# The attention mask as 32 extra operand columns, and PSUM banks given out in order of time

## The chip, the cores and the metric

The kernel runs on one core of one Trainium2 chip. The metric is the device time of one execution in microseconds (us), as the median of several runs; lower is better. The profile is one more execution with the hardware profiler on; its rows are what all durations here are read from. In them PE is TensorE (the matrix engine), PEld its loading of weights, DVE is VectorE, ACT is ScalarE, POOL is GpSimd, and SP is the engine that issues the DMAs.

## The reference

One layer of an encoder on 1024 tokens of width 1024: a half-step SwiGLU FFN, a mixer with two head groups (a gated MLP and an attention over low-rank latents), a second half-step FFN and a final norm.

```python
x = x + 0.5 * swiglu(rmsnorm(x, ffn1_norm), w_gate, w_up, w_down)      # hidden 2816
h = rmsnorm(x, mix_norm) @ w_in        # u 512 | v 512 | c_q 256 | c_kv 128 | k_rope 32
y_a = gmlp_mixer(u, v, ...)
y_b = mla_mixer(c_q, c_kv, k_rope, ...)                                # 8 heads, 96 wide
x = x + concat(rmsnorm(y_a), rmsnorm(y_b)) @ w_out
x = x + 0.5 * swiglu(rmsnorm(x, ffn2_norm), ...)
x = rmsnorm(x, final_norm)
```

The attention is causal in chunks of 64 tokens. A query block has 128 tokens, which is two chunks, and the mask is applied before the softmax:

```python
mask = k_chunk[None, :] <= q_chunk[:, None]
s = jnp.einsum('bqhd,bkhd->bhqk', qb, k)
s = jnp.where(mask[None, None], s, -1e30)
p = jax.nn.softmax(s, axis=-1)
```

In a query block t, keys beyond its 128 tokens are never computed. What the mask must still shut out is one quarter of the diagonal block: the first 64 queries against the last 64 keys.

## The kernel before

All matrix products run in a split form: an operand is held as a high part and a low part (names ending in h and l), and a product is three matmuls, high by high, high by low and low by high. The three lines of such a product stand beside each other in the profile (L963, L964, L965 for the scores).

The program goes through these stages, in this order of time: FFN 1 gate and up (0 to about 500 us), FFN 1 down, the input projection and the gated MLP, the latent stage, the attention (about 844 to 1035 us), the output projection, FFN 2 gate and up (from about 1127 us), FFN 2 down, final norm.

- The FFN products use a Strassen scheme. Gate and up weights come in units; a unit has products P1 to P7 (L438), whose weights are sums of weight quarters (S1 to S4, built by DVE at L409 and split at L423 on ACT and L424 on DVE) and whose moving operands are sums of token quarters (T1 to T4, B11, B21, B22, built by DVE at L368 to L373 and split at L360 on ACT and L361 on DVE). At the start of each FFN the eight token tiles are normalized (L291, DVE), transposed on PE (L286) and copied out (L350, ACT); the T sums need the last of the eight tiles.
- The latent stage (latent_tile, one per token tile of 128) makes queries (L864 to L866) and keys and values (L871 to L873), scales them on DVE (L897 to L899) and rotates the rope columns on POOL (L763 to L767, L901). The tile qn of a token tile has 8 heads by 128 columns, of which 96 are used; kn likewise.
- The attention takes one head h at a time in query pairs. head_T transposes four token tiles of a head (L947) and evicts them as qh, ql, kh, kl (L951 on ACT, L952 on DVE), with 96 rows. scores makes one query block's scores in PSUM with L963 to L965, one group of three for each 512 keys, then adds the mask with one more matmul, L966: its weights are a row of 64 ones and 64 zeros (mrow), its moving operand a row of 64 times -1e30 (mneg), both bf16, and it is added to the last 64 columns. Then DVE takes the row maximum (L968), ACT the exponential (L970), PE transposes the result (L993), which ACT and DVE split (L276, L277); weighted multiplies by the values (L1002, L1003), and folded finishes a pair of blocks (L1014, L1016).

What sets the order: the steps are written out by hand in the code, and a tile scheduler with a timeline of its own (schedule_with_timeline_sim) then places each instruction on its engine's queue, by the dependences between tiles. Each engine runs its queue in order. PSUM has 8 banks. Which bank a PSUM tile gets is fixed before that, by place: a dry pass runs through the program with a clock that counts 1 for a matmul or transpose and 0.01 for any other instruction, and notes when each tile is first and last used. In the kernel before, place takes the tiles in the order of size by lifetime and gives each the bank with the longest free gap, where gaps beyond REACH (160) count as equal and the lowest bank wins. Two tiles that follow each other in a bank are a dependence for the scheduler: the later tile's first matmul waits until the earlier tile is copied out.

## Time and profile before

| what | value |
|---|---|
| median of 3 runs | 1804.01 us (1801.94 to 1806.21) |
| the profiled execution | 1804.58 us, of which 1802.8 us span |
| PE busy | 1731.7 us, 96% of the span |
| DVE busy | 1122.5 us, 62% |
| ACT busy | 750.3 us, 42% |
| POOL busy | 124.9 us, 7% |
| mean granted clock of PE | 0.98 |

The span is the time from the first to the last instruction; 1.8 us lie around it. The granted clock is a share of TensorE's full 2.4 GHz: at 1.00 a 512-column matmul follows the one before it after 0.23 us, and in a stretch at the lower of its two levels, 1.2 GHz, after 0.43 us. A window whose mean clock is, say, 0.90 holds a piece at the lower level. A matmul's duration (0.39 us for 512 columns) is longer than this pace, since matmuls overlap; what one costs a busy PE is the step from its start to the next start.

### The profile page before, as it was taken

What the parts mean: (1) busy time and instruction counts of PE and PEld (TensorE: products, weight loads), DVE (VectorE), ACT (ScalarE), POOL (GpSimd) and SP (SyncE); (2) the same over time, 40 slices, a digit from 0 to 9 for tenths busy, and PEclk for the clock granted to TensorE, in tenths of its full rate; (3) what the DMA queues carried; (4) which work ended last, traced back from release to release, by engine and by line L of the source; (5) the groups of instructions that cost most, each with busy time, mean ns of one, the idle gap of its engine ahead of it and who ended that gap; (6) DMA issues with size and microseconds to landing.
All of it is one profiled execution on the core that took longest, in us unless ns stands there. A gap on an engine that the chain in (4) does not pass through costs nothing.

```text
span 1802.8 us, 21101 instructions
## 1 busy us (share of the span) xinstructions
PE 1731.7 (96%) x8196; PEld 1444.9 (80%) x8196; DVE 1122.5 (62%) x1481; ACT 750.3 (42%) x1139; POOL 124.9 (7%) x242
## 2 busy tenths in 40 slices
PE   6799999999999999997999999889999999999988
PEld 5688888888888888896888888668888888888876
DVE  6875466654687667458676544665556655658753
ACT  6533233334343353355666733433233333433442
POOL 2000000000000004225000500000000000000000
PEclk9899999999999999998999899989999999999999
DMA  6132423225834520300000452131323222783431
GB/s 204 59 117 88 135 93 117 88 94 210 292 129 158 192 88 20 109 13 1 1 1 7 142 174 71 53 118 58 134 101 111 88 95 87 245 308 102 158 121 47
DMA packets 123493, 199.51 MB, mean 111 GB/s; under 512 B 11008, under 2 KB 57600, under 8 KB 123392
## 3 DMA queue, kind: packets, MB, share of 16 engines
q1 hardware_dynamic: 122816, 197.11, 32.0%
q8 instruction: 64, 1.05, 0.2%
q10 hardware_dynamic: 576, 1.05, 0.2%
q14 instruction: 37, 0.30, 0.1%
HBM read 143.07 MB, written 55.05 MB: 110 GB/s over the span
## 4 chain that ended last, share of the span: by engine, by line
PE 91%; DVE 4%; ACT 2%; DMA 1%; SPq 1%; issue 1%; POOL 1%; POOLq 0%; ACTq 0%; DVEq 0%
PE psum L438 45%; PE psum L569 8%; PE psum L570 8%; PE psum L567 7%; PE psum L693 2%; PE psum L691 2%; PE psum L692 2%; PE psum L1093 2%; PE psum L1091 2%; PE psum L1090 2%; PE psum L993 2%; PE psum L963 1%; PE psum L286 1%; PE psum L1002 1%; PE psum L1003 1%; PE psum L965 1%
## 5 line engine op out<-in xcount | busy, mean ns | idle before, releaser
L454 DVE TENSOR_TENSOR P_b<-psum,P_b 128x1024 f32<-128x1024 f32 x33 | 40.3, 1222 | 62.8 <-PE psum L438 62.7
L454 DVE TENSOR_TENSOR P_a<-psum,P_a 128x1024 f32<-128x1024 f32 x33 | 40.3, 1221 | 55.6 <-PE psum L438 55.5
L968 DVE TENSOR_REDUCE nm<-psum 128x1 f32<-128x128 f32 (+3 forms) x64 | 47.8, 753 | 27.9 <-PE psum L966 19.8
L444 ACT COPY P_a<-psum 128x1024 f32<-128x1024 f32 x33 | 33.5, 1014 | 68.6 <-PE psum L438 68.6
L444 ACT COPY P_b<-psum 128x1024 f32<-128x1024 f32 x33 | 33.5, 1014 | 68.1 <-PE psum L438 68.1
L455 ACT ACTIVATE P_a<-P_a 128x512 f32<-128x512 f32 x33 | 20.9, 634 | 96.8 <-DVE P_a L454 96.5
L455 ACT ACTIVATE P_b<-P_b 128x512 f32<-128x512 f32 x33 | 20.9, 633 | 96.4 <-DVE P_b L454 96.3
L277 DVE TENSOR_TENSOR pl<-psum,ph 128x384 fp32r<-128x384 f32 (+1 forms) x80 | 48.8, 629 | 11.6 <-ACT ph L276 11.3
L970 ACT ACTIVATE p<-psum,nm 128x128 f32<-128x128 f32 (+3 forms) x64 | 47.9, 749 | 18.9 <-DVE nm L968 17.1
L963 PE MATMUL psum<-kh,qh 96*128 96x512 f32 (+2 forms) x96 | 41.4, 431 | 11.8 <-ACT qh L951 8.1
L257 POOL TENSOR_TENSOR r_fin<-ms_fin,mhalf 128x1 f32<-128x1 f32 x8 | 6.0, 754 | 643.6 <-DVE ms_fin L255 643.6
L1090 PE MATMUL psum<-woh,yh 128*128 128x512 f32 x128 | 50.5, 397 | 0.0
L1091 PE MATMUL psum<-wol,yh 128*128 128x512 f32 x128 | 50.1, 393 | 0.0
L276 ACT CAST ph<-psum 128x384 fp32r<-128x384 f32 (+1 forms) x80 | 41.6, 550 | 9.0 <-PE psum L993 7.9
L438 PE MATMUL psum<-xT2h_f,S2h_b 128*128 128x512 f32 x88 | 35.4, 402 | 10.1 <-ACT S2h_b L423 10.1
L993 PE MATMUL psum<-ident,p 128*128 128x128 f32 x288 | 43.5, 280 | 1.4 <-ACT p L970 1.2
L1002 PE MATMUL psum<-ph,vv 128*128 128x256 f32 x160 | 44.7, 305 | 0.1
L1003 PE MATMUL psum<-pl,vv 128*128 128x256 f32 x160 | 43.5, 301 | 0.3 <-DVE pl L277 0.3
L257 POOL TENSOR_TENSOR r_m<-ms_m,mhalf 128x1 f32<-128x1 f32 x8 | 5.6, 704 | 551.3 <-DVE ms_m L255 551.3
L1093 PE MATMUL psum<-woh,yl 128*128 128x512 f32 x128 | 43.5, 395 | 0.0
L438 PE MATMUL psum<-xT2l_f,S2h_a 128*128 128x512 f32 x88 | 35.1, 399 | 8.3 <-DVE xT2l_f L361 8.3
L438 PE MATMUL psum<-xT1l_f,S1h_b 128*128 128x512 f32 x88 | 34.7, 396 | 6.0 <-DVE xT1l_f L361 6.0
(519 smaller groups left out, 5717.8 us busy)
## 6 DMA issues: line engine op xcount, KB each, us to landing
raw_a<-in_ffn_w_gate SPq DMA_DIRECT2D x22, 512.0 KB, 4.2
raw_a<-in_ffn_w_up SPq DMA_DIRECT2D x22, 512.0 KB, 5.3
hd<-hS_a SPq DMA_DIRECT2D x44, 256.0 KB, 2.2
raw_b<-in_ffn_w_gate SPq DMA_DIRECT2D x22, 512.0 KB, 4.1
raw_b<-in_ffn_w_up SPq DMA_DIRECT2D x22, 512.0 KB, 5.2
hd<-hS_b SPq DMA_DIRECT2D x44, 256.0 KB, 2.2
aS_a<-hd SPq DMA_DIRECT2D x20, 512.0 KB, 3.9
wB_a<-in_ffn_w_down SPq DMA_DIRECT2D x20, 512.0 KB, 5.4
```

Of the source, the lines that this page charges most:

```text
L438: mm(o, lhs[:, 4 * m + k, :], rhs[:, k, :], start=pn in FIRST and n == 0, stop=n == 11, skip_group_check=True)
L444: nc.scalar.copy(ev[u, pn], bk)
L454: nc.vector.tensor_tensor(c, bk, c, op=ALU.add)
L567: mm(banks[t], hh[:, j, tl], dh[:, j, :], start=pn in DOWN_FIRST and c == 0 and j == 0, stop=False, skip_group_check=True)
L569: mm(banks[t], hh[:, j, tl], dl[:, j, :], start=False, stop=False, skip_group_check=True)
L570: mm(banks[t], hl[:, j, tl], dh[:, j, :], start=False, stop=c == 5, skip_group_check=True)
L993: nc.tensor.transpose(ps[:, i * P:(i + 1) * P], prs[j][:, c * P:(c + 1) * P], ident)
L1002: mm(acc[:, 0:256], mx["vv"][c][:, h, :], hi, start=i == 0, stop=False)
L1003: mm(acc[:, 0:256], mx["vv"][c][:, h, :], lo, start=False, stop=i == len(pts) - 1)
L1090: mm(pe[e], yh[:, k, :], wh[:, es], start=k == 0, stop=False)
L1091: mm(pe[e], yh[:, k, :], wl[:, es], start=False, stop=False)
L1093: mm(pe[e], yl[:, k, :], wh[:, e * 512:(e + 1) * 512], start=False, stop=k == KD - 1)
```

## The change

Two things are changed.

First, the mask. The L966 matmul goes, with its constants. Queries and keys get the 32 spare columns of their tiles filled: in token tile t, column t of the 32 holds 1 in the first 64 query tokens (0 elsewhere), and -1e30 in the last 64 key tokens (0 elsewhere). All other spare columns hold 0. A query block times a key block then adds -1e30 just where both are of the same token tile, the query in its first half and the key in its second. The columns are copied from two constants (qmark, kmark) by POOL, one copy of 128 x 8 x 32 for each qn and each kn: 16 copies, and four memsets at the start. The transposes of head_T, their evictions and the score matmuls work on 128 rows rather than 96; their count and their free sizes stay.

Second, the PSUM banks. place gives them out to the PSUM tiles in the order of first use, and the gap is not cut at REACH: a tile gets the bank that has been free longest. SBUF is placed as before.

PE has 8070 instructions where it had 8198, POOL 264 where it had 247; DVE, ACT and SP have as many as before. Line numbers of the changed kernel are higher by 3 up to the latent stage, by 5 to 7 behind it.

```diff
@@ place: the bank map @@
-def place(bufs, blocks, grain):
+def place(bufs, blocks, grain, in_time=False):
...
     reach = np.full(n, REACH)
     order = sorted(range(n), key=lambda i: (-size[i] * (last[i] - first[i] + 30.0), i))
+    if in_time:
+        reach[:] = 1e9
+        order.sort(key=lambda i: (first[i], i))
...
-        self.at = {"sb": place(dry.bufs["sb"], floats // GRAIN, GRAIN), "ps": place(dry.bufs["ps"], 8, 1)}
+        self.at = {"sb": place(dry.bufs["sb"], floats // GRAIN, GRAIN), "ps": place(dry.bufs["ps"], 8, 1, True)}
@@ constants @@
-    mrow = nc.const([1, P], "mrow", BF16)
-    nc.gpsimd.memset(mrow, 0.0)
-    nc.gpsimd.memset(mrow[:, 0:64], 1.0)
-    mneg = nc.const([1, 64], "mneg", BF16)
-    nc.gpsimd.memset(mneg, -1e30)
+    spare = P - DQ
+    qmark, kmark = (nc.const([P, NT * spare], n) for n in ("qmark", "kmark"))
+    for mark, half, v in ((qmark, slice(0, 64), 1.0), (kmark, slice(64, P), -1e30)):
+        nc.gpsimd.memset(mark, 0.0)
+        nc.gpsimd.memset(mark[half, 0:(NT - 1) * (spare + 1) + 1:spare + 1], v)
@@ latent_tile @@
-        q_t = tile_([P, H, P], f"qn{t}", F32)[:, :, 0:DQ]
-        k_t = tile_([P, H, P], f"kn{t}", F32)[:, :, 0:DQ]
+        q_all = tile_([P, H, P], f"qn{t}")
+        k_all = tile_([P, H, P], f"kn{t}")
+        q_t, k_t = q_all[:, :, 0:DQ], k_all[:, :, 0:DQ]
+        for a, mark in ((q_all, qmark), (k_all, kmark)):
+            m = mark[:, t * spare:(t + 1) * spare].unsqueeze(1)
+            nc.gpsimd.tensor_copy(a[:, :, DQ:P], m.to_broadcast([P, H, spare]))
...
-        mx["q"][t], mx["k"][t], mx["vv"][t] = q_t, k_t, v_t
+        mx["q"][t], mx["k"][t], mx["vv"][t] = q_all, k_all, v_t
@@ head_T @@
-            mx["qk", h] = [tile_([DQ, S], f"{n}{h}", F32R) for n in ("qh", "ql", "kh", "kl")]
+            mx["qk", h] = [tile_([P, S], f"{n}{h}", F32R) for n in ("qh", "ql", "kh", "kl")]
...
-                nc.tensor.transpose(ps[0:DQ, i * 512 + t * P:i * 512 + (t + 1) * P], src[4 * half + t][:, h, :], ident)
+                nc.tensor.transpose(ps[:, i * 512 + t * P:i * 512 + (t + 1) * P], src[4 * half + t][:, h, :], ident)
...
-            pv = ps[0:DQ, i * 512:(i + 1) * 512]
-            nc.scalar.activation(hi[:, cs], pv, AF.Copy, scale=col[0:DQ])
-            nc.vector.scalar_tensor_tensor(lo[:, cs], pv, col[0:DQ], f(hi[:, cs]), op0=ALU.mult, op1=ALU.subtract)
+            pv = ps[:, i * 512:(i + 1) * 512]
+            nc.scalar.activation(hi[:, cs], pv, AF.Copy, scale=col)
+            nc.vector.scalar_tensor_tensor(lo[:, cs], pv, col, f(hi[:, cs]), op0=ALU.mult, op1=ALU.subtract)
@@ scores @@
-            last = n <= c0 + 512
...
-            mm(ps[:, cs], ql[:, tl], kh[:, cs], start=False, stop=not last)
-        mm(ps[:, n - 64:n], mrow, mneg, start=False, stop=True)
+            mm(ps[:, cs], ql[:, tl], kh[:, cs], start=False, stop=True)
```

On PE, in the attention (head 3 in both; L963 to L966 before are L969 to L971 after; p and ident are the transposes of the softmax), a query block of the kernel before:

```order
L963 MATMUL psum<-kh_7553,qh_7549 128x384
L964 MATMUL psum<-kl_7555,qh_7549 128x384
L965 MATMUL psum<-kh_7553,ql_7552 128x384
L966 LDWEIGHTS mrow
L966 MATMUL psum<-mneg,mrow 128x64
L993 MATMUL psum<-ident,p_6_7816 128x128
L993 MATMUL psum<-ident,p_7_7829 128x128
L993 MATMUL psum<-ident,p_6_7816 128x128
```

and of the changed kernel:

```order
L969 MATMUL psum<-kh_7569,qh_7565 128x384
L970 MATMUL psum<-kl_7571,qh_7565 128x384
L971 MATMUL psum<-kh_7569,ql_7568 128x384
L954 MATMUL psum<-ident,qn_7181 128x128
L954 MATMUL psum<-ident,qn_7358 128x128
L954 MATMUL psum<-ident,qn_7424 128x128
L954 MATMUL psum<-ident,qn_7492 128x128
```

The weight load and matmul of the mask stood between the scores and the next transposes, and are gone; the key and query transposes have 128 rows.

On PE, at the start of FFN 1, the transposes of token tiles 6 and 7 (xn_f_381 and xn_f_401) in the kernel before, tile 6's at place 53 of the queue and tile 7's here, among unit 1's matmuls (A11h_a_258):

```order
L438 MATMUL psum<-xB21h_f_226,A12h_a_337 128x512
L438 MATMUL psum<-xB21l_f_227,A12h_a_337 128x512
L286 MATMUL psum<-ident,xn_f_401 128x128 x8
L438 MATMUL psum<-xB11h_f_218,A11h_a_258 128x512
L438 MATMUL psum<-xB11l_f_219,A11h_a_258 128x512
```

and in the changed kernel, where the two tiles are xn_f_384 and xn_f_404:

```order
L289 MATMUL psum<-ident,xn_f_384 128x128 x8
L289 MATMUL psum<-ident,xn_f_404 128x128 x8
L441 MATMUL psum<-xB21h_f_229,A12h_a_340 128x512
L441 MATMUL psum<-xB21l_f_230,A12h_a_340 128x512
L441 MATMUL psum<-xB21h_f_229,A12l_a_343 128x512
```

Tile 7's eight transposes were at place 77, behind 23 of unit 1's matmuls, and are at place 54 now, right behind tile 6's.

On DVE, at the same place, from the first T sum (L368) on; P_a_458 is unit 1's product P1 plus P2, and xB22l and xT2l are the low parts of the B22 and T2 operands. Before:

```order
L368 TENSOR_TENSOR t_f_462<-b_f_314,b_f_310 128x1024 x2
L369 TENSOR_TENSOR t_f_465<-t_f_462,b_f_153 128x1024
L373 TENSOR_TENSOR b_f_310<-b_f_310,b_f_153 128x1024
L361 TENSOR_TENSOR xB22l_f_500<-b_f_314,xB22h_f_499 128x1024 x2
L369 TENSOR_TENSOR t_f_465<-t_f_462,b_f_153 128x1024
L373 TENSOR_TENSOR b_f_310<-b_f_310,b_f_153 128x1024
L361 TENSOR_TENSOR xT3l_f_492<-t_f_462,xT3h_f_491 128x1024
L370 TENSOR_TENSOR b_f_156<-b_f_156,t_f_465 128x1024
L454 TENSOR_TENSOR P_a_458<-psum,P_a_458 128x1024
L361 TENSOR_TENSOR xT3l_f_492<-t_f_462,xT3h_f_491 128x1024
L361 TENSOR_TENSOR xT2l_f_471<-t_f_465,xT2h_f_470 128x1024
```

and in the changed kernel:

```order
L371 TENSOR_TENSOR t_f_465<-b_f_317,b_f_313 128x1024 x2
L372 TENSOR_TENSOR t_f_468<-t_f_465,b_f_156 128x1024
L376 TENSOR_TENSOR b_f_313<-b_f_313,b_f_156 128x1024
L372 TENSOR_TENSOR t_f_468<-t_f_465,b_f_156 128x1024
L376 TENSOR_TENSOR b_f_313<-b_f_313,b_f_156 128x1024
L364 TENSOR_TENSOR xT3l_f_495<-t_f_465,xT3h_f_494 128x1024
L373 TENSOR_TENSOR b_f_159<-b_f_159,t_f_468 128x1024
L364 TENSOR_TENSOR xT3l_f_495<-t_f_465,xT3h_f_494 128x1024
L364 TENSOR_TENSOR xT2l_f_474<-t_f_468,xT2h_f_473 128x1024
L364 TENSOR_TENSOR xT1l_f_486<-b_f_313,xT1h_f_485 128x1024
L373 TENSOR_TENSOR b_f_159<-b_f_159,t_f_468 128x1024
L364 TENSOR_TENSOR xB22l_f_503<-b_f_317,xB22h_f_502 128x1024 x2
```

The two xB22l and the addition to P_a stood ahead of the first xT2l and are behind it now (the addition still further on).

On ACT, at the start of FFN 2, the casts for unit 0's weight sums (S2h_b_11153 and S4h_b_11260). Before:

```order
L360 CAST xT4h_f_11140<-b_f_10324 128x1024 x2
L455 ACTIVATE P_b_11184<-P_b_11184 128x512
L360 CAST xB22h_f_11132<-b_f_10754 128x1024 x2
L423 CAST S4h_b_11260<-S_b_11147 128x1024
L423 CAST S2h_b_11153<-S_b_11062 128x1024
L423 CAST S3h_b_11225<-S_b_11150 128x1024
```

and in the changed kernel, where they are S2h_b_11106 and S4h_b_11213:

```order
L363 CAST xT4h_f_11093<-b_f_10277 128x1024 x2
L363 CAST xB22h_f_11085<-b_f_10707 128x1024 x2
L458 ACTIVATE P_b_11137<-P_b_11137 128x512
L426 CAST S2h_b_11106<-S_b_11015 128x1024
L426 CAST S4h_b_11213<-S_b_11100 128x1024
L426 CAST S3h_b_11178<-S_b_11103 128x1024
```

S2's cast has moved ahead of S4's.

## Rows read from the trace of the kernel before

**Rows 1.** The page of the profile: busy time of PE with its share of the span, and the chain of work that ended last, by engine.

```profile
PE 1731.7 (96%) x8196; PEld 1444.9 (80%) x8196; DVE 1122.5 (62%) x1481; ACT 750.3 (42%) x1139; POOL 124.9 (7%) x242
...
PE 91%; DVE 4%; ACT 2%; DMA 1%; SPq 1%; issue 1%; POOL 1%; POOLq 0%; ACTq 0%; DVEq 0%
```

**Rows 2.** The span in windows of 50 us: start and end of the window, its length, then the busy time (and instructions) of PE, PEld, DVE, ACT and POOL, then PE's granted clock, the DMA share and GB/s.

```profile
50.00:100.00 50.00, 39.52 (x164) 31.33 (x163) 41.66 (x40) 22.95 (x25) 0.00 (x0) 0.90 0.24 79
800.00:850.00 50.00, 41.94 (x227) 38.67 (x226) 43.87 (x133) 32.46 (x90) 22.29 (x46) 0.93 0.01 1
900.00:950.00 50.00, 49.78 (x347) 42.38 (x346) 34.89 (x70) 33.51 (x77) 4.08 (x21) 1.00 0.00 1
950.00:1000.00 50.00, 49.70 (x348) 42.46 (x347) 33.89 (x65) 35.07 (x79) 4.73 (x17) 1.00 0.09 27
1150.00:1200.00 50.00, 33.90 (x142) 27.15 (x141) 40.06 (x36) 21.92 (x24) 0.00 (x0) 0.83 0.16 53
```

**Rows 3.** The waits of PE from 862 to 1000 us (total us, times, longest); this is the only line that the view gives.

```profile
PE psum L963 <- ACT p L970: 0.2, 1, 0.2
```

**Rows 4.** The timeline of PE in the attention: start, duration, line, operands, rows, columns.

```profile
923.43 0.39 PE L965 MATMUL psum<-kh,ql 96*128 96x512 f32 x1
923.75 0.20 PE L966 MATMUL psum<-mneg,mrow 1*128 1x64 bf16 x1
923.88 0.38 PE L963 MATMUL psum<-kh,qh 96*128 96x256 f32 x1
924.10 0.28 PE L964 MATMUL psum<-kl,qh 96*128 96x256 f32 x1
924.22 0.28 PE L965 MATMUL psum<-kh,ql 96*128 96x256 f32 x1
...
925.12 0.39 PE L965 MATMUL psum<-kh,ql 96*128 96x512 f32 x1
925.35 0.49 PE L993 MATMUL psum<-ident,p 128*128 128x128 f32 x3
```

**Rows 5.** The mask matmul alone (L966) in three stretches: window, length, busy time and count on PE and on PEld, clock, DMA.

```profile
840.00:860.00 20.00, 1.15 (x5) 0.49 (x5) 0.57 0.00 1
860.00:1000.00 140.00, 10.09 (x51) 4.63 (x51) 0.99 0.03 10
1000.00:1030.00 30.00, 1.71 (x9) 0.75 (x8) 0.83 0.36 115
```

**Rows 6.** The weight loads of the transposes: of queries with 96 columns (L947), and of the softmax with 128 (L993). Durations in ns are least, median and longest.

```profile
L947 PEld LDWEIGHTS psum<-ident,qn x64: 124/126/203, 833.3 to 1003.8; 128*96 128x96 f32 x64
...
L993 PEld LDWEIGHTS psum<-ident,p x288: 137/141/230, 861.6 to 1042.6; 128*128 128x128 f32 x144
```

**Rows 7.** The timeline of all engines at the start of FFN 1, the rows that the T sums hang on; in brackets the idle time of the engine before the row, and what ended it.

```profile
44.48 1.03 PE L286 MATMUL psum<-ident,xn_f 128*128 128x128 f32 x8
...
46.23 2.36 DVE L368 TENSOR_TENSOR t_f<-b_f,b_f 128x1024 f32<-128x1024 f32 x2 [3.99 <-ACT b_f L350]
...
50.77 2.35 DVE L361 TENSOR_TENSOR xB22l_f<-b_f,xB22h_f 128x1024 fp32r<-128x1024 f32 x2
...
57.59 1.22 DVE L454 TENSOR_TENSOR P_a<-psum,P_a 128x1024 f32<-128x1024 f32 x1
...
61.13 0.80 PE L438 MATMUL psum<-xT2l_f,S2h_a 128*128 128x512 f32 x1 [8.35 <-DVE xT2l_f L361]
...
63.26 1.22 DVE L361 TENSOR_TENSOR xT2l_f<-t_f,xT2h_f 128x1024 fp32r<-128x1024 f32 x1
```

**Rows 8.** The same at the start of FFN 2.

```profile
1172.04 1.99 ACT L360 CAST xB22h_f<-b_f 128x1024 fp32r<-128x1024 f32 x2 [0.50 <-DVE xT2l_f L361]
...
1177.71 1.05 ACT L423 CAST S4h_b<-S_b 128x1024 fp32r<-128x1024 f32 x1 [3.68 <-DVE S_b L409]
1178.85 1.05 ACT L423 CAST S2h_b<-S_b 128x1024 fp32r<-128x1024 f32 x1
...
1179.93 1.23 DVE L424 TENSOR_TENSOR S2l_b<-S_b,S2h_b 128x1024 fp32r<-128x1024 f32 x1 [0.39 <-ACT S2h_b L423]
...
1181.82 0.63 PE L438 MATMUL psum<-xT2h_f,S2l_b 128*128 128x512 f32 x1
```

**Rows 9.** The timeline of POOL before and in the latent stage: an instruction with one input of 128 x 128, one with two inputs of 128 x 256, and a memset.

```profile
747.75 0.54 POOL L786 TENSOR_SCALAR late<-late 128x128 f32<-128x128 f32 x1
...
794.63 0.62 POOL L901 TENSOR_TENSOR kn<-late,r_qk 128x256 f32<-128x256 f32 x1 [11.74 <-DVE r_qk L267]
...
827.41 0.20 POOL L988 MEMSET ph<- 128x128 f32 x1 [1.57 <-PE psum L693]
```

**Rows 10.** The timeline of all engines where head 0's scores begin.

```profile
853.75 0.69 ACT L951 ACTIVATE qh<-psum,gqcol 96x512 fp32r<-96x512 f32 x1 [2.27 <-DVE rs L897]
...
854.48 0.58 PE L963 MATMUL psum<-kh,qh 96*128 96x256 f32 x1 [8.09 <-ACT qh L951]
```

**Rows 11.** The timeline of POOL and DVE in the latent stage: the same small DVE line (L266) alone, and while POOL is at work.

```profile
804.04 0.17 DVE L266 SCALAR_TENSOR_TENSOR t_qk<-t_qk,ssq 128x16 f32<-128x16 f32 x1
...
806.35 1.12 POOL L763 TENSOR_TENSOR rt<-qn,late 128x256 f32<-128x256 f32 x1 [1.17 <-DVE qn L898]
...
806.80 0.70 DVE L266 SCALAR_TENSOR_TENSOR t_c<-t_c,ms_c 128x2 f32<-128x2 f32 x1
```

**Rows 12.** The page's group of the softmax exponential on ACT: busy us and mean ns, then the idle time before it and what ended most of it.

```profile
L970 ACT ACTIVATE p<-psum,nm 128x128 f32<-128x128 f32 (+3 forms) x64 | 47.9, 749 | 18.9 <-DVE nm L968 17.1
```

## The prediction

> **What bounds the kernel now.** I read the page first, then the span in windows, then the waits and the timeline of the stages that the change touches. PE is busy for 96% of the span and holds 91% of the chain that ended last [rows 1], so only what shortens PE's queue, or a stretch in which PE stands still, can show in the time. The windows tell the two apart [rows 2]. In the attention (900 to 1000 us) PE is busy for 99.5 of 100 us at full clock, with DVE at 69% and ACT at 69%. Its waits from 862 to 1000 us come to 0.2 us in all [rows 3]. That stage is bound by PE's queue, and an instruction taken out of it is time won as long as DVE and ACT keep up. At three places PE does stand still: 50 to 100 us (39.5 of 50 busy, mean clock 0.90), the latent stage before the attention (41.9 of 50, DVE 43.9 of 50), and the start of FFN 2 (33.9 of 50, mean clock 0.83). There the chain through DVE and ACT decides, and the new bank order moves instructions at all three.
>
> **The mask matmul, gone.** Its duration, 0.20 us, is not its price, since matmuls overlap; the price is what the starts show [rows 4]. From L965 with 512 columns to the mask are 0.32 us, where to a transpose (925.12 to 925.35) they are 0.23: +0.09. From the mask to the next matmul are 0.13 us. The matmul after it is late once more: L963 with 256 columns takes 0.22 us to the next start, where the same size takes 0.12 (924.10 to 924.22): +0.10. Together 0.32 us for each query block. The 96-row matmuls themselves show no such loss: 96 rows to 128 rows is the plain 0.23 above, so the change to 128 rows neither wins nor costs anything there.
>
> There are 64 masks; the three windows record 65, one being cut by an edge. 51 lie between 860 and 1000 us, where PE is the bound: 50 x 0.32 = 16.0 us. The other 14 lie at the start (5) and the end (9) of the attention, where PE also waits for others: 14 x 0.32 = 4.5 us, of which I take half, 2.2 us [rows 5]. The upper end is 64 x 0.32 = 20.5 us. The lower end is that DVE and ACT become the bound at once. They are busy 69% in the mean, and taking a tenth of PE's time out brings them to some 77%; in order queues with such a load start to wait for each other, and what I see in this is a loss of about a fifth of the 16.0. So 12.8 + 2.2 = 15 us won, between 5 and 20.5.
>
> The transposes of head_T load 128 columns where they loaded 96: 126 ns against 141 ns [rows 6], 128 times 0.015 = 1.9 us of PEld at most. It lies under the matmuls, and I cost it at nothing; if it were all exposed it would be 1.9 us.
>
> **FFN 1's start.** The tile-7 transposes start at 44.48 us, and the T sums on DVE start behind them and their copies at 46.23, after 3.99 us of idle time [rows 7]. In the new order these transposes no longer stand behind 23 matmuls of 0.23 us, 5.3 us. They still need tile 7's normalized values, and two copies and one table load on ACT, so I take 3.4 us of the 3.99 as won: more than the idle time cannot be. Behind the first sum, three DVE instructions of 1.14 us (two xB22l, starting at 50.77, and the addition at 57.59) go behind the first xT2l, but only one of the three goes behind the second xT2l, which the P6 product needs as well. PE waits 8.35 us for the first xT2l, and the second (63.26 us) is ready when PE, at the lower clock, gets to it. So the second decides: 3.4 + 1.1 = 4.5 us. From then on PE is dense for hundreds of us, so this carries through to the end. Bounds: 1 us, if the copies on ACT, with a table load among them now, eat the lead, and 7 us, if all of 3.99 and the 3 x 1.14 are won.
>
> **FFN 2's start.** Ahead of the last tile's transposes stood 60 matmuls of units 0 and 1 on PE, and now stand 55: 5 x 0.23 = 1.1 us earlier, which the later place of S4's sum on DVE (one instruction, 1.14 us) gives back. But PE's wait for S2h ends sooner: S2's cast stood behind S4's cast, which came at 1177.71 after 3.68 us of idle time; now it follows the B22 casts (1172.04 plus 1.99 us) and P1's activation. PE then has four matmuls to do before it needs S2l, whose subtraction came at 1179.93 on DVE after 0.39 us of waiting for S2h, and it used S2l at 1181.82 [rows 8]. It can have S2l 0.4 us earlier plus the 1.1 us of the earlier start, ready at about 1179.7 rather than used at 1181.82: 2 us won. Bounds: 4 us won (all of the 3.68), 1 us lost (S4's sum later on).
>
> **The latent stage.** 16 POOL copies are new and the trace has no such copy. The nearest row is the instruction of 128 x 256 with two inputs, 0.62 us; twice a memset of 128 x 128 gives 0.40, twice the one-input instruction 1.08 [rows 9]. I take 0.62: about 10 us on POOL, against 22.3 of 50 busy us in the fullest window, and with idle gaps like the 11.74 us ahead of that row. On POOL's queue the copies stand ahead of the rope instructions of later tiles, so a late one delays qn and the transposes that read it. The banks add a wait: the key matmuls of tiles 5, 6 and 7 now follow each other in one pair of banks, and each needs the copies of the one before on ACT and DVE. But PE is idle here anyway. Head 0's scores begin when ACT's qh is done (853.75, PE's wait of 8.09 us), and ACT waited for DVE's scaling of tile 7 [rows 10]; DVE's order from tile 5 on has the same instructions ahead of it. I take 2 us lost, between 1 won and 10 lost.
>
> How much DVE loses to POOL is shown by one line: L266 takes 0.17 us alone, but 0.70 us when it starts within POOL's L763 (806.35 plus 1.12 = 807.47), and ends at 807.50, with it [rows 11]. A copy may so hold DVE until it ends; seven of the 16 stand among the dense part of the latent stage, 7 x 0.62 = 4.3 us at worst, and half of that is the 2 us above.
>
> The Trainium skill, in "SBUF — State Buffer", section "Who interferes with whom", states it as a rule: a DVE instruction with two SBUF inputs contends with a GpSimd instruction that reads SBUF, and the one that started first keeps the port until its end. The trace agrees in the L266 row above. By this rule a copy, which reads SBUF, can hold DVE where a memset can't.
>
> **Elsewhere** the banks only move instructions within stretches in which PE is dense already (FFN units, down products, output projection); I cost that at nothing, since a dense PE covers it. If that cover failed it would show as new PE waits on copies, which is the last rival below.
>
> **The sum.** -15 - 4.5 - 2 + 2 = -19.5 us. The profiled execution took 1804.6 us (1802.8 of span and 1.8 around it), so 1785.1; it lies 0.6 us above the median of the runs, which gives 1784.5 us.
>
> **The rivals.**
> - *All of it is won* (18%). DVE and ACT keep up with a denser PE, the first xT2l decides in FFN 1, and a piece at the lower clock goes with the shorter wait: -20.5 - 7 - 4 - 1 = -32.5, which gives 1771.5 us. For it: no waits of PE in 862 to 1000 us. Against it: DVE's 69% is a mean, and queues in order need not fill the gaps.
> - *The attention becomes bound by DVE and ACT* (14%). Then 5 us are won there: -5 - 4.5 - 2 + 2 = -9.5, 1794.5 us. For it: the row maximum and the exponential follow each scores group at once, so that they are as late as before. Against it: each engine has 30% to spare.
> - *POOL holds DVE* (7%), the mechanism of L266 with all 16 copies on the path: +10 instead of +2, and with half of the gain in the attention gone the time is 1804.0 - 7.5 - 6.5 + 10 = 1800. Against it: a copy waits for nothing but its buffer, and much of POOL's time is idle.
> - *New waits for banks* (8%), the one that ends slower. With banks given by time alone, a score group takes the bank free longest even where its last owner is still waiting for ACT; PE, in order, stands behind it with everything that follows. Place: the scores, 64 query blocks. Price: a wait of one exponential, 0.75 us [rows 12], at each block is 48 us; against the 22 us of gains it decides from a mean new wait of 22 / 64 = 0.34 us. With 0.5 us a block: 1804 - 22 + 32 = 1814 us. For it: ACT's exponential is the last reader of these banks. Against it: the wait of PE for it is 0.2 us now, and a longer free time of a bank makes such waits rarer.
>
> **Chances.** The forecast holds 53%. A measurement of this kernel tells no change from a change of 0.2%, 3.6 us. Faster by more than that: the forecast, the first two rivals, and a third of the POOL rival: 87%. Within it: 6%, from the POOL rival and mild new waits. Slower: 7%. The range for 8 in 10 reaches from 1770 (most of the first rival) to 1800 us (the second and third); the forecast's own range is 1779 to 1792.
>
> **What would show it right or wrong.** In the new profile there is no step longer than 0.24 us from the last 512-column score matmul to the next start, and PE is still above 97% busy in the attention; if its waits there name ACT's exponential or DVE's row maximum, the second rival holds, and if they name them in front of the first score matmul of a block, the last. FFN 1's first xT2 matmul starts near 54 us, PE's wait ahead of it is below 4 us, and PE is dense from 64 us at the latest, rather than 65. In FFN 2, PE starts xT2h some 4 us sooner and stops again for S2l. In the latent stage PE's wait for qh stays at about 8 us; if it grows by more than 5, the copies or the bank pair cost more than said. The forecast is wrong if the attention's length, from the first to the last score, has shrunk by less than 10 us.

## The result and the profile after

The changed kernel takes 1781.09 us (median of 4 runs, 1780.10 to 1782.07) against 1803.18 us for the kernel before in the same comparison: a ratio of 0.9875, 95% interval 0.9858 to 0.9892, or 22.1 us less. In a second comparison it took 1781.18 us against 1802.17 (0.9880, 0.9864 to 0.9897). The forecast was 1784.5 us, within 1770 to 1800.

The profiled execution has a span of 1780.0 us, 22.8 us less than before. The page's line of busy times and its chain by engine, to be held against [rows 1]:

```profile
PE 1709.0 (96%) x8132; PEld 1436.5 (81%) x8132; DVE 1120.3 (63%) x1481; ACT 746.5 (42%) x1139; POOL 132.2 (7%) x259
...
PE 90%; DVE 4%; ACT 2%; DMA 1%; SPq 1%; issue 1%; POOL 0%; POOLq 0%; ACTq 0%; DVEq 0%
```

PE's busy time has fallen by 22.7 us (1731.7 to 1709.0), and its idle time, span less busy, has stayed: 71.1 us before, 71.0 after. So PE's queue takes less time, in part because less of it ran at the lower clock (below), and the stops that the new bank order removed in one place have come back in another. The windows, with the columns of [rows 2], show where:

```profile
50.00:100.00 50.00, 44.56 (x186) 35.42 (x185) 41.72 (x41) 21.40 (x24) 0.00 (x0) 0.97 0.30 100
800.00:850.00 50.00, 37.62 (x205) 34.64 (x203) 41.61 (x121) 30.10 (x78) 22.93 (x46) 0.91 0.00 1
900.00:950.00 50.00, 49.35 (x370) 45.99 (x368) 38.43 (x74) 36.46 (x85) 4.12 (x22) 1.00 0.00 1
950.00:1000.00 50.00, 46.31 (x346) 43.00 (x343) 36.75 (x75) 41.29 (x98) 19.60 (x30) 1.00 0.28 90
```

From 50 to 100 us PE is 5 us busier. From 800 to 850 it is 4.3 us less busy. In the attention it starts 716 matmuls in 100 us where it started 695, and yet it is no longer quite full: 95.7 us of 100.

To compare stages of kernels that start at different times I use three marks on PE, which stand in every kernel: A is the first product of xB22h with S4h in FFN 1 (PE always waits 1.10 us for ACT there), B is head 0's score matmul behind PE's wait for qh [rows 10], D is the first product of xT2h with S2h in FFN 2. All times in us, from one profiled execution of each kernel, "until A" counted from the span's start and the last column from D to the span's end:

| kernel | until A | A to B | B to D | D to end | span |
|---|---|---|---|---|---|
| before | 80.46 | 774.02 | 325.47 | 622.85 | 1802.8 |
| changed | 76.91 | 777.83 | 301.01 | 624.25 | 1780.0 |
| changed, once more | 77.63 | 777.82 | 301.31 | 622.24 | 1779.0 |
| mask alone | 80.52 | 774.41 | 300.76 | 623.31 | 1779.0 |
| banks alone | 82.48 | 778.17 | 315.99 | 622.96 | 1799.6 |
| no mask at all | 81.71 | 774.04 | 300.93 | 623.82 | 1780.5 |
| banks alone, one fill more | 76.81 | 778.20 | 319.07 | 623.92 | 1798.0 |
| mixed banks | 78.31 | 774.44 | 300.98 | 622.27 | 1776.0 |

Before to changed: -3.55 until A, +3.81 from A to B, -24.46 from B to D, +1.40 from there. The sum is the 22.8 us.

A single execution is not exact to a tenth. Six kernels of this study that have the old banks and the old SBUF places up to A reach it between 80.32 and 82.00 us, and the two executions of the changed kernel differ by 0.7 us until A and by 2.0 from D on; from A to B all kernels with the same banks there agree within 0.6. B is not quite the same place of PE's queue either: the kernel before has one query block ahead of it, the others of the table have two. That block, 1.1 us with its mask in the kernel before (859.85 to 860.95, at the lower clock), lies behind B in the first row alone.

The attention, B to D, comes first. The changed kernel's PE timeline at the place that answers to [rows 4]: the last score matmul of 512 columns, its step to the transposes, and a block of 256 columns.

```profile
908.17 0.40 PE L971 MATMUL psum<-kh,ql 128*128 128x512 f32 x1
908.40 1.07 PE L998 MATMUL psum<-ident,p 128*128 128x128 f32 x8
909.23 0.36 PE L969 MATMUL psum<-kh,qh 128*128 128x256 f32 x1
...
909.55 0.28 PE L971 MATMUL psum<-kh,ql 128*128 128x256 f32 x1
909.67 0.27 PE L998 MATMUL psum<-ident,p 128*128 128x128 f32 x1
```

The step of 0.32 us behind the scores is 0.23 (908.17 to 908.40), and 0.12 behind 256 columns (909.55 to 909.67). The waits of PE from 862 to 1000 us, where [rows 3] had one line of 0.2 us, are now:

```profile
PE psum L998 <- ACT p L975: 1.8, 3, 1.0
PE psum L969 <- DVE kl L959: 1.5, 1, 1.5
PE psum L1008 <- DVE pl L280: 0.9, 1, 0.9
PE psum L969 <- DVE pl L280: 0.8, 2, 0.5
```

With two more of 0.4 and 0.2 us that is 5.6 us: PE does run into DVE and ACT. How close they are now shows in the page's group of the exponential (L970 before, [rows 12]): ACT's idle time ahead of it has gone from 18.9 to 7.7 us.

```profile
L975 ACT ACTIVATE p<-psum,nm 128x128 f32<-128x128 f32 (+3 forms) x64 | 48.1, 755 | 7.7 <-DVE nm L973 7.2
```

The denser PE alone does not do this. From B to the first matmul of the output projection PE is idle for 3.1 us before, 3.5 with the mask alone and with no mask at all, 3.0 with the banks alone, 3.8 with mixed banks (old banks in this stage), and 6.5 in both executions of the changed kernel. So some 3 us of waiting need the missing masks and the new banks together. With the mask alone ACT's idle time ahead of the exponential is still 14.9 us.

FFN 1's start in the changed kernel, beside [rows 7]: tile 7's transposes, and PE's two stops for xT2l.

```profile
40.70 1.06 PE L289 MATMUL psum<-ident,xn_f 128*128 128x128 f32 x8 [1.21 <-DVE xn_f L294]
...
56.02 0.80 PE L441 MATMUL psum<-xT2l_f,S2h_a 128*128 128x512 f32 x1 [2.90 <-DVE xT2l_f L364]
...
61.70 0.50 PE L441 MATMUL psum<-xT2l_f,S2h_a 128*128 128x512 f32 x1 [1.13 <-DVE xT2l_f L364]
```

The stop of 8.35 us has become two of 2.90 and 1.13. Mark A is 3.55 us earlier.

Where head 0's scores begin, beside [rows 10]:

```profile
850.50 0.58 PE L971 MATMUL psum<-kh,ql 128*128 128x256 f32 x1 [11.50 <-DVE ql L959]
...
854.74 0.58 PE L969 MATMUL psum<-kh,qh 128*128 128x256 f32 x1 [3.01 <-ACT qh L958]
```

Before, a first stop stood ahead of the one in [rows 10]:

```profile
844.80 0.58 PE L963 MATMUL psum<-kh,qh 96*128 96x256 f32 x1 [2.90 <-DVE kl L952]
```

PE was 3.55 us ahead at A and waits 14.51 us in two stops here, where it waited 10.99 in two (2.90 and 8.09): the lead is gone by 854.74 (854.48 before).

FFN 2's start, beside [rows 8]; first PE's two stops before, then the changed kernel:

```profile
1168.65 1.22 PE L438 MATMUL psum<-xT1l_f,S1h_b 128*128 128x512 f32 x2 [6.03 <-DVE xT1l_f L361]
...
1179.95 0.79 PE L438 MATMUL psum<-xT2h_f,S2h_b 128*128 128x512 f32 x1 [10.07 <-ACT S2h_b L423]
```

```profile
1144.46 0.97 PE L441 MATMUL psum<-xT1l_f,S1h_b 128*128 128x512 f32 x2 [3.58 <-DVE xT1l_f L364]
...
1152.27 2.35 DVE L364 TENSOR_TENSOR xB22l_f<-b_f,xB22h_f 128x1024 fp32r<-128x1024 f32 x2
...
1154.65 1.04 ACT L426 CAST S2h_b<-S_b 128x1024 fp32r<-128x1024 f32 x1 [4.29 <-DVE xB22l_f L364]
...
1155.75 0.80 PE L441 MATMUL psum<-xT2h_f,S2h_b 128*128 128x512 f32 x1 [10.32 <-ACT S2h_b L426]
```

S2's cast has nothing of ACT's own in front of it any more, but it waits 4.29 us for the two xB22l on DVE, whose end (1152.27 + 2.35 = 1154.62) frees it. PE waits 10.32 us for S2h, where the kernel before shows 10.07. The stop in front of it, for xT1l, is 3.58 us where it was 6.03, so that PE stands still for 13.9 us here and stood for 16.1 before. With the mask alone and with mixed banks it is 16.1 again, with the banks alone 14.1: this stop is shortened by the bank order.

### The profile page after: what moved, and what is told of

Read it like the earlier page. It is cut to its first block, busy times and chain, and to the rows that moved or that the text cites. A ratio compares the mean times of both kernels' runs of the same rounds, so it can differ in the third digit from the quotient of the medians.

```text
span 1780.0 us, 20994 instructions
## 1 busy us (share of the span) xinstructions
PE 1709.0 (96%) x8132; PEld 1436.5 (81%) x8132; DVE 1120.3 (63%) x1481; ACT 746.5 (42%) x1139; POOL 132.2 (7%) x259
## 4 chain that ended last, share of the span: by engine, by line
PE 90%; DVE 4%; ACT 2%; DMA 1%; SPq 1%; issue 1%; POOL 0%; POOLq 0%; ACTq 0%; DVEq 0%
PE psum L441 45%; PE psum L572 8%; PE psum L573 8%; PE psum L570 8%; PE psum L694 2%; PE psum L696 2%; PE psum L695 2%; PE psum L1095 2%; PE psum L1098 2%; PE psum L1096 2%; PE psum L998 1%; PE psum L969 1%; PE psum L289 1%; PE psum L1008 1%; PE psum L970 1%; PE psum L1007 1%
## 5 line engine op out<-in xcount | busy, mean ns | idle before, releaser
L447 ACT COPY P_b<-psum 128x1024 f32<-128x1024 f32 x33 | 33.4, 1013 | 68.3 <-PE psum L441 68.3
L280 DVE TENSOR_TENSOR pl<-psum,ph 128x512 fp32r<-128x512 f32 (+1 forms) x80 | 48.4, 627 | 6.0 <-ACT ph L279 5.8
L279 ACT CAST ph<-psum 128x512 fp32r<-128x512 f32 (+1 forms) x80 | 42.3, 561 | 7.3 <-PE psum L998 7.3
L971 PE MATMUL psum<-kh,ql 128*128 128x512 f32 (+2 forms) x96 | 33.7, 358 | 11.5 <-DVE ql L959 11.5
L969 PE MATMUL psum<-kh,qh 128*128 128x512 f32 (+2 forms) x96 | 38.4, 400 | 6.0 <-ACT qh L958 3.0
```

The source lines that it names most:

```text
L447: nc.scalar.copy(ev[u, pn], bk)
```

## The experiments

### Which of the two edits makes the gain

The changed kernel with the old bank rule:

```diff
-  "ps": place(dry.bufs["ps"], 8, 1, True)
+  "ps": place(dry.bufs["ps"], 8, 1)
```

> The changed kernel with the PSUM banks placed as in the kernel before: mask columns alone. Theory (the mask matmul costs PE 0.32 us each in a stretch that PE bounds): 15 to 20 us below the kernel before, about 1783 to 1788 us, the attention from head 0's first scores to the last scores 18 to 22 us shorter. Rival (the bank order gave most of the gain, by fewer waits of PE): 1796 us or more. FFN 1's start: theory says that its 3.5 us came with the banks, so PE reaches the first xT2l product at about 61 us again.

Measured: 1781.52 us, ratio 0.9881 (0.9866 to 0.9896), a little below the range of the theory. The mask alone gives the whole gain.

The kernel before with the new bank rule, and its mask matmuls kept:

```diff
-  "ps": place(dry.bufs["ps"], 8, 1)
+  "ps": place(dry.bufs["ps"], 8, 1, True)
```

> The kernel before with the PSUM banks in order of time, mask matmul kept. Theory: 0 to 5 us below the kernel before (1798 to 1803 us), all of it outside the attention, whose length is unchanged to within 2 us since PE waits only 0.2 us there. Rival (banks gave the gain): 1783 to 1790 us and a shorter attention.

Measured: 1801.40 us, ratio 0.9994 (0.9984 to 1.0003). The banks by themselves make no difference that can be told from none. The table says that they do move the stages: 4.15 us more from A to B, in the changed kernel 3.81 more. From B to D the profile is 9.5 us shorter than that of before, where I had expected the attention's length to stay within 2: some 5 us of it are a stretch at the lower clock that does not come here (below), 1.1 the query block that has moved ahead of B, and 2.0 the stops at FFN 2's start. Until A the banks gave -3.55 us in the changed kernel, and here nothing: 82.48 us, 0.5 above the latest of the old kernels. That is taken up again below.

The kernel before without the mask matmul, with 96 rows. It leaves the mask out altogether, so that queries also see the keys that the mask hides:

```diff
-  mm(ps[:, cs], ql[:, tl], kh[:, cs], start=False, stop=not last)
-  mm(ps[:, n - 64:n], mrow, mneg, start=False, stop=True)
+  mm(ps[:, cs], ql[:, tl], kh[:, cs], start=False, stop=True)
```

> The kernel before without the mask matmul, with nothing in its place (the mask is left out, 96 rows, no mask columns, old banks). Theory (columns and 128 rows cost almost nothing): within 3 us of the kernel with mask columns and old banks, that is 1781 to 1788 us. Rival (the 16 POOL copies or the 128-row operands cost several us): 5 us or more below that kernel.

Measured: 1780.63 us, ratio 0.9879 (0.9864 to 0.9893), as the mask alone. So what the change puts in the mask's place (32 more rows in transposes, evictions and scores, and the 16 POOL copies) costs nothing that can be measured, and the gain is what goes with the 64 mask matmuls, most of it their price. From B to D PE is busy for 306.24 us before and 281.35 us here, with 63 of the masks in between. Of the 24.9 us, 6.2 are the lower clock's (9.9 us lost to it before, 3.7 here; 5.0 of the difference is a stretch at the end of the attention, below), and 0.4 the query block's scores that have moved ahead of B. So 18.2 us are left, 0.29 us a mask.

### What a mask matmul costs, and why

The mask's bf16 operands on 128 rows, all zeros but the first row:

```diff
-  mrow = nc.const([1, P], "mrow", BF16)
-  mneg = nc.const([1, 64], "mneg", BF16)
+  mrow = nc.const([P, P], "mrow", BF16)
+  mneg = nc.const([P, 64], "mneg", BF16)
```

> The kernel before with the same mask matmul, but its bf16 operands have 128 rows (zeros but for the first) instead of 1. Theory (the price of a mask is the change of the row count, 0.09 us into it and 0.10 us out of it, and only the rest is the matmul): the step from the last 512-column score matmul to the mask falls from 0.32 to about 0.23 us and the matmul after the mask is no longer late, so 64 x 0.19 = 12 us less at most, 1791 to 1796 us. Rival (the price comes from the other data type, or from any short matmul with weights of its own): the steps stay at 0.32 and 0.22, about 1803 us.

Measured: 1792.32 us, ratio 0.9941 (0.9924 to 0.9957), about half of the gain. Its PE timeline:

```profile
920.19 0.40 PE L965 MATMUL psum<-kh,ql 96*128 96x512 f32 x1
920.43 0.20 PE L966 MATMUL psum<-mneg,mrow 128*128 128x64 bf16 x1
920.47 0.36 PE L963 MATMUL psum<-kh,qh 96*128 96x256 f32 x1
920.67 0.28 PE L964 MATMUL psum<-kl,qh 96*128 96x256 f32 x1
920.79 0.29 PE L965 MATMUL psum<-kh,ql 96*128 96x256 f32 x1
920.92 0.20 PE L966 MATMUL psum<-mneg,mrow 128*128 128x64 bf16 x1
```

The step into the mask is the plain 0.24 us again (0.32 before), and the step out 0.04 (0.13 before). But the matmul behind takes 0.20 to its successor, where its size takes 0.12. A mask of 128 rows costs 0.04 + 0.08 or 0.09 = 0.13 us. Is that rest the change from bf16 to fp32r? The same with fp32r operands:

```diff
-  mrow = nc.const([P, P], "mrow", BF16)
-  mneg = nc.const([P, 64], "mneg", BF16)
+  mrow = nc.const([P, P], "mrow", F32R)
+  mneg = nc.const([P, 64], "mneg", F32R)
```

> The kernel before, with the mask's two operands in fp32r instead of bf16 and with 128 rows (zeros but for row 0); the number of mask matmuls and the bank rule are unchanged. In the run with bf16 operands of 128 rows the matmul after the mask still started 0.08 to 0.09 us late. Theory type: that remainder is the change of type from bf16 to fp32r, so here a mask costs its own 0.04 us and hardly more, some 0.05 us instead of 0.32 us (0.13 us with 128 rows of bf16), and the time is 1783 to 1786 us. Rival: the remainder belongs to any switch to another pair of operands inside an accumulation; then the step stays 0.13 us and the time 1791 to 1793 us.

Measured: 1792.05 us, ratio 0.9946 (0.9931 to 0.9961). My theory of the type falls: nothing changed. The same type with one row:

```diff
-  mrow = nc.const([1, P], "mrow", BF16)
-  mneg = nc.const([1, 64], "mneg", BF16)
+  mrow = nc.const([1, P], "mrow", F32R)
+  mneg = nc.const([1, 64], "mneg", F32R)
```

> The kernel before, with the mask's two operands in fp32r instead of bf16 and still with one row. Theory: the price of a mask is the sum of two parts, 0.18 to 0.19 us for the change of rows on the way in and out and 0.08 to 0.09 us for the change of type; without the second a mask costs 0.23 to 0.24 us instead of 0.32 us and the time is 1796 to 1799 us. Rival: the change of type alone sets the 0.32 us of a one-row mask; then the time is near 1783 to 1786 us. Second rival: with one row the two parts overlap, so that nothing is won, 1801 to 1804 us.

Measured: 1807.62 us, ratio 1.0032 (1.0019 to 1.0045), 6.1 us slower than before, where all three expectations said faster or the same. This miss explains the price. Its PE timeline, then the weight loads (PEld) of the same stretch, and then the weight loads of the kernel before:

```profile
921.20 0.28 PE L965 MATMUL psum<-kh,ql 96*128 96x256 f32 x1
921.41 0.29 PE L966 MATMUL psum<-mneg,mrow 1*128 1x64 f32 x1
921.63 0.39 PE L963 MATMUL psum<-kh,qh 96*128 96x256 f32 x1
921.85 0.28 PE L964 MATMUL psum<-kl,qh 96*128 96x256 f32 x1
```

```profile
921.09 0.19 PEld L965 LDWEIGHTS psum<-kh,ql 96*128 96x128 f32 x1
921.41 0.18 PEld L966 LDWEIGHTS psum<-mneg,mrow 1*128 1x128 f32 x1
921.63 0.19 PEld L963 LDWEIGHTS psum<-kh,qh 96*128 96x128 f32 x1
921.74 0.19 PEld L964 LDWEIGHTS psum<-kl,qh 96*128 96x128 f32 x1
```

```profile
923.74 0.09 PEld L966 LDWEIGHTS <-mrow 1*128 1x128 bf16 x1 [0.36 <-issue]
923.87 0.19 PEld L963 LDWEIGHTS psum<-kh,qh 96*128 96x128 f32 x1
```

Among the scores a weight load starts 0.11 us ahead of its matmul, beside the matmul in front: L964's load at 921.74, its matmul at 921.85. The one-row mask's load starts with its matmul (both at 921.41), and so does the load behind it (921.63). So at a change between 1 and 96 rows nothing overlaps, and the weight load stands in PE's path. In fp32r it takes 0.18 us and in bf16 0.09; the steps from the mask to the next matmul are 0.22 and 0.13, and the difference of 0.09 us, times 64, is 5.8 of the 6.1 us. The Trainium skill, "TensorEngine Tiling (Array Packing)", section "Tiling Modes", says that changing the tiling mode drains TensorE. For 1 against 96 rows the trace fits this, at 0.17 to 0.20 us a mask in bf16 (0.29 to 0.33 against 0.12 to 0.13, table below), though no row names a mode; between 96 and 128 rows it shows no such stop (0.23 us, [rows 4]).

The rest, 0.13 us, could be one more weight load that 64 columns are too few to cover, or a switch. To tell, the mask of 128 rows was written over 256 columns, with zeros in 192 of them:

```diff
-  mm(ps[:, n - 64:n], mrow, mneg, start=False, stop=True)
+  w0 = max(c0, n - 256)
+  m0 = 256 - (n - w0)
+  mm(ps[:, w0:w0 + 256], mrow, mneg[:, m0:m0 + 256], start=False, stop=True)
```

> The kernel before, with the mask's bf16 operands on 128 rows as in the earlier run, and written over 256 score columns instead of 64 (zeros in the 192 others). Theory load: what is left of a mask's price at 128 rows, 0.13 us, is the weight load of the matmul behind it, which 64 columns (0.04 us) don't cover and 256 columns (0.12 us) do; so the four times wider mask costs the same 0.12 to 0.13 us, the matmul behind it starts without lateness, and the time is 1791 to 1793.5 us. Rival: the lateness of 0.08 to 0.09 us belongs to the switch itself; then a wide mask costs 0.12 us and 0.08 us, and the time is 1796 to 1799 us.

Measured: 1789.63 us, ratio 0.9930 (0.9915 to 0.9945). Four times the columns cost hardly anything; the switch falls. That the time is even 2.7 us below the narrow mask's is not the width: from B to D the lower clock costs 3.6 us here and 7.1 there. (This kernel also has one constant fill more and so other SBUF places, which the next section comes to.)

```profile
920.59 0.28 PE L966 MATMUL psum<-kh,ql 96*128 96x256 f32 x1
920.71 0.28 PE L969 MATMUL psum<-mneg,mrow 128*128 128x256 bf16 x1
920.75 0.37 PE L1005 MATMUL psum<-ph,vv 128*128 128x256 f32 x1
920.96 0.28 PE L1006 MATMUL psum<-pl,vv 128*128 128x256 f32 x1
```

The recorded starts kept their pattern, though, 0.04 and then 0.21 us, where I had expected 0.12 and 0.12. What counts is the sum of the two, 0.25 us less one plain step of 0.12, which is 0.13 again. So in this stream a mask costs about 0.13 us, be it 64 columns or 256. A weight load that nothing covers would do this. The Trainium skill, "TensorE: Matmul & The Clock Gate", section "Back-to-back issue gap", says of a stream of weight loads and matmuls that the spacing is set by the load and the matmul together. That the load is the cause here is not shown: the loads in these timelines take 0.19 us (scores) and 0.09 us (one-row mask in bf16), and neither is the 0.13.

Per mask, from the steps at 25 to 29 masks of each kernel between 865 and 990 us (the median of them), and from PE's busy time from B to D: less what the lower clock cost there (busy time times one less the granted clock, in windows of 5 us: from 3.3 to 9.9 us), less the same of the kernel without a mask (277.7 us), less 0.44 us for the query block that lies behind B with a mask and ahead of it without, divided by 63:

| mask | busy time, us | steps, us | median, us |
|---|---|---|---|
| 1 row, fp32r | 0.39 | 0.42 | 1807.62 |
| 1 row, bf16 (before) | 0.29 | 0.33 | 1801.56 to 1803.18 |
| 128 rows, bf16 | 0.12 | 0.13 | 1792.32 |
| 128 rows, fp32r | 0.13 | 0.12 | 1792.05 |
| 128 rows, bf16, 256 columns | 0.15 | 0.13 | 1789.63 |
| in the spare columns (mask alone) | 0.00 | | 1781.52 |

### What the bank order does

Until A the banks gave -3.55 us in the changed kernel and nothing alone, although the PSUM tiles get the same banks in both. What differs is SBUF. The rule for SBUF is untouched, but its ties go by planned times, and one constant fill more at the start of the program shifts these by 0.01: worked out from the planner's own rule, 692 of 1845 SBUF tiles of the changed kernel have another place than before. To test this, the kernel before, masks and all, with the new banks and one fill written twice, which gives every tile up to planned time 400 the place of the changed kernel:

```diff
-  "ps": place(dry.bufs["ps"], 8, 1)
+  "ps": place(dry.bufs["ps"], 8, 1, True)
   nc.gpsimd.memset(mhalf, -0.5)
+  nc.gpsimd.memset(mhalf, -0.5)
```

> The kernel before, mask matmuls and all, with the banks in order of time and with one constant's fill written twice. The second fill moves the planner's clock by 0.01, which breaks ties in the placement of SBUF tiles otherwise: up to planned time 400 every tile then has the place that it has in the changed kernel. Theory: the earlier start of the first feed-forward comes from the bank order together with these SBUF places, and the mask has no part in it; then the mark of the first feed-forward (80.46 us before, 82.48 us with the bank order alone, 76.91 us in the changed kernel) stands at 76.5 to 77.5 us, and the time, with the latent stage some 4 us longer, is 1797 to 1802 us. Rival: the mask's columns have a part in it; then the mark stays near 82 us.

Measured: 1799.62 us, ratio 0.9984 (0.9975 to 0.9993), and mark A, with the stops of the changed kernel, at 76.81:

```profile
55.93 0.51 PE L442 MATMUL psum<-xT2l_f,S2h_a 128*128 128x512 f32 x1 [2.88 <-DVE xT2l_f L365]
...
61.61 0.50 PE L442 MATMUL psum<-xT2l_f,S2h_a 128*128 128x512 f32 x1 [1.05 <-DVE xT2l_f L365]
...
76.81 0.50 PE L442 MATMUL psum<-xB22h_f,S4h_a 128*128 128x512 f32 x1 [1.10 <-ACT P_a L448]
```

So the mask has no part in FFN 1's start. It takes the bank order and these SBUF places together: the places with the old banks give 80.52 (mask alone) and 81.12 (the wide mask, whose extra fill gives it the same places here), the banks with the old places 82.48, and both together 76.81, 76.91 and 77.63.

From A to B the table splits cleanly: 774.0 to 774.4 us wherever the latent stage has the old banks, 777.8 to 778.2 wherever it has the new ones. Can one have the first without the second? The changed kernel, with banks in order of time only for the PSUM tiles planned before 400:

```diff
-  reach[:] = 1e9
-  order.sort(key=lambda i: (first[i], i))
+  early = first < 400.0
+  reach[early] = 1e9
+  order.sort(key=lambda i: (0, first[i], i) if early[i] else (1, 0, 0))
```

> The changed kernel, with banks in order of time only for the PSUM tiles whose planned start lies before 400 (the start of the first feed-forward), and by the old rule for all later ones. Theory: the bank rule gives 3.5 us at the start of the first feed-forward and takes 3.8 us back in the latent stage, and the two can be had apart; then the feed-forward's mark stands near 77 us as in the changed kernel, the first scores start near 850.5 us after the mark's gain, and the time is 1777 to 1779 us against 1781. Rival: the loss in the latent stage comes from the gain itself (work moved early pushes other work late), whatever the later banks are; then the time is 1780.5 to 1782 us.

Measured: 1777.55 us, ratio 0.9870 (0.9853 to 0.9886), with A at 78.10 (2.4 us won where I expected 3.5, a difference within the scatter of mark A) and A to B 774.45. Since the changed kernel's time was from another comparison, both were run again side by side:

> The changed kernel once more, beside the next one on the same chip: 1780 to 1782.5 us.

> The kernel with banks in order of time up to planned time 400 only, once more, beside the changed kernel on the same chip. Theory: the difference between the two earlier medians, 3.5 us, and between their spans, 4.4 us, is the loss in the latent stage that the old rule avoids; then it is 2.5 to 4.5 us faster than the changed kernel here too. Rival: the two differ by the chip; then they agree within 1.5 us.

Measured: 1781.18 us (1780.12 to 1781.61) for the changed kernel and 1777.61 (1776.64 to 1777.77) for the mixed banks, ratios 0.9880 and 0.9860 (0.9845 to 0.9875). The two intervals against the kernel before overlap, but the runs side by side don't: 3.6 us, the fastest kernel of this study. Its scores begin behind stops of 4.25 and 7.64 us, much as before (2.90 and 8.09); the second is this:

```profile
852.75 0.58 PE L970 MATMUL psum<-kh,qh 128*128 128x256 f32 x1 [7.64 <-ACT qh L959]
```

What ends the latent stage is DVE's queue: ACT's qh, for which PE waits, waits itself for DVE's rs. In the 50 us that begin 713.1 us behind A, DVE gets 39.66 us of work done in the changed kernel and 42.93 with the mixed banks, windows of each in turn:

```profile
790.00:840.00 50.00, 47.62 (x260) 44.22 (x258) 39.66 (x126) 35.19 (x94) 23.78 (x48) 1.00 0.00 1
```

```profile
791.40:841.40 50.00, 47.04 (x260) 44.25 (x258) 42.93 (x132) 34.54 (x94) 26.60 (x51) 1.00 0.00 1
```

These 3.3 us are nearly all of the 3.4 by which A to B differs. In the same 50 us behind A DVE's work is 39.7 to 39.8 us with the new banks (banks alone, one fill more, the changed kernel once more) and 42.9 with the old ones (before, mask alone, no mask). So the banks are the cause; which single bank makes DVE late, and by what wait, was not narrowed down.

### The stretch at the lower clock

In the profiled execution of before, PE's granted clock is at its lower level for ten us at the end of the attention, behind three waits of 1.9 us in sum, while ACT splits the output weights:

```profile
1000.00:1010.00 10.00, 8.77 (x65) 7.48 (x64) 7.14 (x14) 9.65 (x21) 9.51 (x12) 1.00 0.73 232
1010.00:1013.00 3.00, 2.19 (x11) 1.41 (x11) 2.09 (x4) 3.00 (x11) 3.00 (x5) 1.00 0.30 104
1013.00:1023.50 10.50, 10.50 (x43) 9.03 (x42) 3.94 (x8) 5.69 (x13) 6.84 (x9) 0.52 0.23 77
```

10.5 us at 0.52, close to 1.2 of 2.4 GHz, are 5.0 us lost. The changed kernel has no such stretch at the end of its attention; at the start of the attention, behind the wait for qh, every kernel has one. To see whether the waits bring it, the 16 copies of the weights' high parts were moved from ACT to DVE:

```diff
-  nc.scalar.copy(hi[:, es], raw)
+  nc.vector.tensor_copy(hi[:, es], raw)
```

> The kernel before, with the 16 high-part copies of the output weights moved from ScalarE to VectorE. In the profile of before ScalarE is 9.65 of 10 us busy between 1000 and 1010 us, TensorE waits there for 1.9 us in three waits, and from 1013.2 to 1023.4 us its granted clock is at the lower level, which costs about 5 us. Theory: the waits bring the clock down; with the copies off ScalarE they are shorter than 0.5 us in sum, the lower clock does not come, and the time is 1795 to 1798 us. Rival: the waits have another cause or only move, and the time is 1801 to 1804 us. Second rival: the waits shrink and the lower clock comes all the same, about 1800.5 to 1802 us.

Measured: 1810.50 us, ratio 1.0043 (1.0028 to 1.0057). That is slower than all three expectations, and not the test I wanted: DVE became full instead (9.91 and 10.00 us of 10 busy in the two windows from 1000 us), PE waited 5.2 us in sum, and the clock fell for longer:

```profile
1010.00:1020.00 10.00, 6.95 (x40) 5.58 (x39) 10.00 (x18) 3.50 (x10) 7.83 (x9) 0.81 0.43 155
1020.00:1030.00 10.00, 10.00 (x41) 8.62 (x41) 4.74 (x10) 3.32 (x8) 4.33 (x6) 0.51 0.24 82
```

More waiting, more of the lower clock, here. But the changed kernel waits 3.7 us between 985 and 998 us, and the banks alone 2.3 us between 1005 and 1013, and neither loses the clock there; with one fill more the latter lost 1.5 us to it there. What decides stays open. Nor does all of the 5.0 us stand in the medians: the profiled execution of before had a mean clock of 0.980 and took 1804.6 us, while its 13 runs beside the last four kernels had 0.981 to 0.983 and a median of 1802.2.

## Why the prediction was right, and where it was not

The time came out 3.4 us below the forecast. In the profiled executions a term that the forecast lacks, the lower clock, gave more than that, and the terms that it has were off both ways and cancelled in part. That the sum came so near is partly luck.

**The mask, -15 us: near in sum, with its parts mis-sized.** The price read from the starts, 0.32 us, holds (0.33 by the steps, 0.29 by busy time), and so does "the change to 128 rows neither wins nor costs anything": the mask alone and no mask agree within 1 us. The deduction "of which I take half" for the masks at the ends failed: without the masks all of them are won, 18.2 us of busy time for 0.4 us more of idle time in the attention. The other, "a loss of about a fifth of the 16.0", is 3.2 us, and PE's idle time in the attention did grow by 3.4, which leaves some 15 of the 18.2. But the reason given, DVE and ACT behind a denser PE, accounts for 0.4 us of it; the other 3.0 come only with the new banks, which I had put at nothing there. PE's whole idle time from B to D hides this: it has grown by 1.5 us only, from 19.2 to 20.7 (20.75 is 301.01 less 280.26 busy), since FFN 2's stops became shorter. Beyond the term, the profile won 7.9 us from B to D at the lower clock (9.9 us lost to it before, 1.9 after), 5.0 of them in the stretch at the attention's end, which I had not seen. It stood in [rows 5] as a clock of 0.83 from 1000 to 1030 us, where I read only the count of masks.

**FFN 1, -4.5 us: 3.55 won (2.7 to 5.1 as mark A scatters), for a reason I had only half.** The moved transposes and the two shortened stops came as said, and the second xT2l decides. But "the new bank order" alone does not move them; it needs the SBUF places, which I took as unchanged.

**FFN 2, -2 us: some 2 us won, but not by the mechanism.** PE's two stops there are 2.2 us shorter in sum, 13.9 us instead of 16.1. The step that failed is "now it follows the B22 casts and P1's activation": S2's cast has moved ahead on ACT, but it is released by DVE's xB22l, and the wait for S2h is 0.25 us longer. I read the order of one queue and not the wait that would come last. What became shorter is the stop before it, for xT1l (6.03 to 3.58 us), which the prediction does not price; that the size agrees is luck. The 1.40 us from D to the end are the lower clock's (by the same reckoning as above, 5.5 us of it from D on, 4.1 before), and the changed kernel's second execution does not have them (622.24).

**The latent stage, +2 us: 3.81 lost.** The copies that I charged for take 0.40 us in the median, not 0.62, and cost 0.4 us on the path at most (mask alone, A to B, 774.41 against 774.02). So POOL holding DVE, the rule that the prediction took from the Trainium skill ("SBUF — State Buffer", "Who interferes with whom"), is not what costs here; how long single DVE instructions were held was not gone into. It is the banks, which I had put at nothing there because "PE is idle here anyway". PE is, but with the new banks DVE gets 3.3 us less done in the window before the scores, and DVE ends the stage. That its queue is fed late through the banks is inferred.

**The rivals.** New waits for banks at each score group didn't come: none of the waits above is one of an exponential at each block. The attention bound by DVE and ACT is there in its beginnings, but it takes back 3.4 us, 3.0 of them only with the new banks, and not 10.

**The signs.** Of 47 steps from a 512-column score matmul to the next start, all but one, which has a wait in it, are 0.24 us at most, and PE's stops for xT2l are 2.90 and 1.13 us: as said. The attention is 22.8 us shorter from B to the last score matmul and 15.5 from the first score, whose block has moved ahead of the stops: more than the 10 us that I had named, either way. The first xT2 matmul, at 52.51, says little, since it stood at 52.05 before. PE above 97% in the attention: no, 95.7%. FFN 2's xT2h sooner: no. The wait for qh at 8 us: no, it is 3.0 behind a new one of 11.5. The two stops ahead of the scores grew by 3.5 us in sum; the 5 us that I had named as the mark of a bank pair that costs more were too high, since the banks did cost 3.8.
